# SwiGLU's out-projection as seven block products in a one-core decoder layer

## The chip, the core and the metric

The kernel runs on one core of one Trainium2 chip. The metric is the device time of one execution in microseconds (us), as the median over runs; lower is better. TensorE (PE in the rows) multiplies matrices, VectorE (DVE) and ScalarE (ACT) work element by element, GpSimd (POOL) does some of that too, and SyncE (SP) issues most of the transfers.

## What is computed

One decoder layer over 1024 tokens of width 1024 in float32: RMSNorm, stick-breaking attention with 16 heads, residual; RMSNorm, a SwiGLU network with 2816 hidden columns, residual; a gated add of a per-layer embedding; a last RMSNorm. The part at hand is

```
def swiglu(x, w_in, w_out):
    a, b = jnp.split(x @ w_in, 2, axis=-1)
    return (jax.nn.silu(a) * b) @ w_out
...
h = h + swiglu(rms_norm(h, norm_ffn[i]), ffn_w_in[i], ffn_w_out[i])
gate = jax.nn.sigmoid(rms_norm(h, norm_ple[i]) @ ple_w_gate[i])
```

The change concerns the product with `w_out` (2816 x 1024), called the out-projection below.

## The kernel before

Activations lie transposed: the 128 partitions hold a slice of the width or of the hidden columns, the free dimension holds tokens. Every float32 operand of a matmul is split into two float32r parts, a high part (ScalarE casts the tile) and a low part (VectorE or GpSimd subtracts the high part from the tile). One block product is then three matmuls (`mm3`, lines 126 to 129): high by high, high by low, low by high. A 128 x 1024 split costs one ScalarE and one VectorE instruction, and the VectorE one needs the ScalarE one's result.

The in-projection (lines 843 to 913) runs over 22 hidden tiles `k`; it already computes seven products per tile instead of eight. Its last element-by-element work (`glu`, line 830) multiplies by the sigmoid and stores the activation tile `act_d[k][h]` (128 hidden columns by 512 tokens, `h` is the half of the tokens) to DRAM on SP's queue. For the last tile, `k` = 21, that work is put off into `rest_0` and `rest_1`, which run inside the out-projection.

The out-projection (lines 954 to 988) loops over the two token halves `h` and in each over the 22 hidden tiles `k`. A step loads the 512 KB of weights `w_fo[k]` and the 256 KB of `act_d[k][h]`, splits both (`w_split`, lines 106 to 108: `whi`, `wlo`; `act_split`, lines 626 and 627: `act`), and multiplies them into eight PSUM banks `pm`, one per 128 output columns `m`: 8 x 3 = 24 matmuls of 128 x 512 each. The last two steps of a half are taken bank by bank, and each finished bank gets the residual added (`residual`, line 939, in from DRAM as `h2`) into `hres[m]`. Over both halves that is 2 x 22 x 24 = 1056 matmuls. All of the weights are split twice, once for each half.

The gate projection that follows needs `hres[m]` times its gain, split into `gh[m]` and `gl[m]`, and the sum of squares `acc3` (`parts3`, lines 941 to 952: on ScalarE the high part, line 944, and the square, line 950; on VectorE the low part, line 945; the sum on GpSimd or VectorE, line 952). For the first half of the tokens that runs inside the second half's steps 2 to 9. Five of the eight gate weights `w_g` are split inside the second half too (`WGK`).

The order is written out by hand: under `manual_schedule` every engine executes its instructions in the order in which the program names them, and a tile's buffer is waited for one by one. The pool `xp` has sixteen 512 KB slots (tag X) that hold the split parts.

Of the kernel before, what the change touches and what calls it, by code (L numbers as in the profile page):

```python
# [7 lines left out]
F32 = mybir.dt.float32  # L8
# [24 lines left out]
WGK = [3, 7, 11, 15, 18]  # L33
# [7 lines left out]
def tile_trunk(ctx: ExitStack, tc: tile.TileContext, xT, pT, gains, ident, w_qkv, w_o, w_fi, w_fo, w_g, w_p, outT):  # L41
# [25 lines left out]
    for h in range(2):  # L67
        for k in range(NFF):
            order.append((w_fo[k], KT, k == NFF - 1))
            if h == 1 and k in WGK:  # L70
                order.append((w_g[WGK.index(k)], KT, True))
    for m in range(len(WGK), KT):
        order.append((w_g[m], KT, m < 6))
# [22 lines left out]
    def w_split(k):  # L96
        if k < lim[0] and k in raws:
# [9 lines left out]
            eng = nc.gpsimd if k < N1 or n_fi <= k < n_fi + 2 or k >= len(order) - 3 else nc.vector  # L107
# [514 lines left out]
    def act_split(i):
        if i < 2 * NFF and i not in acts:
            t = araw.pop(i)
            a = duo(xp, f"act{i}", "X", None)
            nc.scalar.copy(a[:, 0, :], t)
            nc.vector.tensor_tensor(a[:, 1, :], t, f(a[:, 0, :]), op=ALU.subtract)  # L627
            acts[i] = a

    with ExitStack() as c2:  # L630
        p2 = c2.enter_context(tc.tile_pool(name="p2", bufs=1, reuse_waits="tile"))

# [210 lines left out]
        for k in range(NFF):  # L843
# [3 lines left out]
            if k >= NFF - 2:  # L847
                for i in range(2):
                    w_load(n_fi + 2 * (k + 2 - NFF) + i)
                act_dma(k + 2 - NFF)  # L850
# [18 lines left out]
            if k == NFF - 1:  # L869
                w_split(n_fi)  # L870
                act_split(0)
# [26 lines left out]
            if k == NFF - 1:  # L898
                act_dma(2)
# [25 lines left out]
        rests = [rest_0, rest_1]  # L925


    p3 = ctx.enter_context(tc.tile_pool(name="p3", bufs=1, reuse_waits="tile"))
    hres = [p3.tile([P, T], F32, name=f"h{m}") for m in range(KT)]
    hh = [p3.tile([P, T], F32R, name=f"gh{m}") for m in range(KT)]  # L930
    hl = [p3.tile([P, T], F32R, name=f"gl{m}") for m in range(KT)]
# [110 lines left out]
    for ri, (c0, n) in enumerate(ranges):  # L1042
# [3 lines left out]
        for m in range(KT):  # L1046
# [3 lines left out]
            for kt in range(KT):  # L1050
                mm3(ps[:, :n], wh[:, kt, :], wl[:, kt, :], hh[kt][:, c0:c0 + n], hl[kt][:, c0:c0 + n], kt == 0, kt == KT - 1)
# [76 lines left out]
```

## Time and profile before

| what | value |
|---|---|
| median of 3 runs | 1380.06 us (1379.49 to 1381.41) |
| profiled execution, its own time | 1380.04 us |
| its span, first to last instruction | 1378.3 us |
| mean granted TensorE clock | 0.996 of full |
| busy, share of the span: PE / DVE / ACT / POOL | 98% / 73% / 44% / 30% |

The profiled execution took what the median run takes, and 1.7 us lie outside its span. Busy shares are averages over stages that have different limits, so each stage is read by itself, from the stretches and the timeline. In the rows below, L108 is line 108; out<-in are the program's names without their numbers; "idle before" is how long the engine stood still before an instruction and what released it. Matmuls overlap: one lasts 389 ns, but the next one starts before it ends.

### The profile page before, as it was taken

The page shows a single profiled execution, that of the slowest core. Times are in us where ns is not written, and L with a number is a line of the kernel's source. Part 1 is how long each engine was busy: PE and PEld are TensorE (multiplying, and loading weights), DVE is VectorE, ACT ScalarE, POOL GpSimd, SP SyncE. Part 2 cuts the span into 40 slices and gives each one's busy share as a digit, 9 for nine tenths or more (in the row PEclk, how much of TensorE's full clock was granted, in tenths as well). Part 3 has the DMA queues.
Part 4 walks back from the last instruction along what each step waited for, and adds up shares of the span by engine and source line. Part 5 has one row for each costly group of instructions (what it writes and reads, how often), then busy time and mean ns, then how long its engine had stood idle before and what let it go on. Part 6 is the DMA issues. An engine that isn't in the chain of part 4 may idle for free. (4 is left out here: it accounts for less than half of the span.)

```text
span 1378.3 us, 17601 instructions
## 1 busy us (share of the span) xinstructions
PE 1353.9 (98%) x6620; PEld 1133.0 (82%) x6620; DVE 1004.1 (73%) x1305; ACT 607.6 (44%) x1082; POOL 408.3 (30%) x280
## 2 busy tenths in 40 slices
PE   8999999999999999999999999999999999999996
PEld 6888888888888888888888888888888888888896
DVE  6878878787887866677878888888884335635675
ACT  6555565656556665443222223222323233534322
POOL 2222221313222401245454544545450000301321
PEclk9999999999999999999999999999999999999998
DMA  5101111110101662442221222212235446455123
GB/s 185 62 16 61 31 48 45 47 47 31 61 31 68 208 237 70 148 143 78 92 92 63 75 92 92 92 62 76 92 138 183 138 143 227 150 181 178 35 72 101
DMA packets 55509, 137.54 MB, mean 100 GB/s; under 512 B 6016, under 2 KB 10496, under 8 KB 55424
## 3 DMA queue, kind: packets, MB, share of 16 engines
q1 hardware_dynamic: 53136, 128.82, 27.2%
q0 software_dynamic: 2016, 7.34, 1.5%
q8 instruction: 52, 0.85, 0.2%
q14 instruction: 33, 0.27, 0.1%
q10 hardware_dynamic: 272, 0.26, 0.1%
HBM read 104.94 MB, written 31.46 MB: 99 GB/s over the span
## 5 line engine op out<-in xcount | busy, mean ns | idle before, releaser
L417 DVE TENSOR_TENSOR_SCAN a<-a,hot 128x128 f32<-128x128 f32 (+7 forms) x128 | 188.8, 1491 | 24.6 <-ACT a L410 24.0
L108 POOL TENSOR_TENSOR wlo<-wraw,whi 128x1024 fp32r<-128x1024 f32 x29 | 72.8, 2516 | 293.3 <-ACT whi L106 117.9
L106 ACT CAST whi<-wraw 128x1024 fp32r<-128x1024 f32 x84 | 88.2, 1051 | 161.8 <-PE b_m L128 144.6
L108 DVE TENSOR_TENSOR wlo<-wraw,whi 128x1024 fp32r<-128x1024 f32 x55 | 69.1, 1257 | 119.6 <-ACT whi L106 119.5
L127 PE MATMUL b_pj<-xh,whi 128*128 128x512 f32 x352 | 140.6, 399 | 0.0
L129 PE MATMUL b_pj<-xh,wlo 128*128 128x512 f32 x352 | 138.7, 394 | 0.4 <-POOL wlo L108 0.4
L128 PE MATMUL b_pj<-xl,whi 128*128 128x512 f32 x352 | 137.8, 391 | 0.0
L440 DVE TENSOR_TENSOR al<-b_tp,ah 128x512 fp32r<-128x512 f32 (+2 forms) x160 | 93.1, 599 | 53.9 <-ACT ah L439 53.5
L439 ACT CAST ah<-b_tp 128x512 fp32r<-128x512 f32 (+2 forms) x160 | 82.0, 522 | 78.7 <-PE b_tp L430 77.8
L410 ACT ACTIVATE a<-b_z 128x128 f32<-128x128 f32 (+2 forms) x192 | 87.0, 491 | 49.0 <-PE b_z L408 47.8
L128 PE MATMUL b_m<-act,whi 128*128 128x512 f32 x264 | 102.8, 389 | 0.4 <-DVE act L627 0.4
L127 PE MATMUL b_m<-act,whi 128*128 128x512 f32 x264 | 102.8, 389 | 0.0
L129 PE MATMUL b_m<-act,wlo 128*128 128x512 f32 x264 | 102.7, 389 | 0.0
L430 PE MATMUL b_tp<-hot,a 128*128 128x128 f32 x576 | 94.3, 273 | 2.5 <-DVE al L440 2.5
L430 PEld LDWEIGHTS b_tp<-hot,a 128*128 128x128 f32 x576 | 72.6, 140 | 25.8 <-DVE al L440 5.5
L129 PEld LDWEIGHTS b_pj<-xh,wlo 128*128 128x128 f32 x352 | 66.0, 188 | 16.2 <-POOL wlo L108 0.5
L128 PEld LDWEIGHTS b_pj<-xl,whi 128*128 128x128 f32 x352 | 66.2, 188 | 8.9
L127 PEld LDWEIGHTS b_pj<-xh,whi 128*128 128x128 f32 x352 | 66.1, 188 | 8.6
L450 PE MATMUL b_av<-ah,V 128*128 128x512 f32 (+2 forms) x160 | 70.7, 442 | 0.0
L952 POOL TENSOR_TENSOR acc<-acc,sq 128x512 f32<-128x512 f32 x10 | 17.6, 1756 | 158.5 <-ACT sq L950 157.8
L832 ACT ACTIVATE sg<-u 128x512 f32<-128x512 f32 x22 | 13.9, 633 | 108.8 <-issue 86.6
L128 PEld LDWEIGHTS b_m<-act,whi 128*128 128x128 f32 x264 | 49.6, 188 | 11.1 <-DVE act L627 0.8
(3040 smaller groups left out, 3745.6 us busy)
## 6 DMA issues: line engine op xcount, KB each, us to landing
fraw<-w_fi SPq DMA_DIRECT2D x44, 512.0 KB, 4.4
wraw<-w_fo SPq DMA_DIRECT2D x44, 512.0 KB, 3.7
wraw<-w_qkv SPq DMA_DIRECT2D x22, 512.0 KB, 3.6
araw<-act SPq DMA_DIRECT2D x44, 256.0 KB, 3.9
h<-h SPq DMA_DIRECT2D x32, 256.0 KB, 3.1
sp<-hl SPq DMA_DIRECT2D x14, 512.0 KB, 3.0
act<-u SPq DMA_DIRECT2D x22, 256.0 KB, 2.2
act<-c SPq DMA_DIRECT2D x22, 256.0 KB, 2.6
```

The source lines that it names most:

```text
L106: nc.scalar.copy(hi[:, :n, :], t[:, :n, :])
L108: eng.tensor_tensor(lo[:, :n, :], t[:, :n, :], f(hi[:, :n, :]), op=ALU.subtract)
L127: nc.tensor.matmul(ps, whi, xhi, start=first, stop=False)
L128: nc.tensor.matmul(ps, whi, xlo, start=False, stop=False)
L129: nc.tensor.matmul(ps, wlo, xhi, start=False, stop=last)
L410: nc.scalar.activation(a[:, c0:c0 + e], z[:, :e], AF.Sigmoid, scale=-SCALE)
L417: nc.vector.tensor_tensor_scan(a[:, L - 1::-1], a[:, L - 1::-1], hot[:, back], 0.0, op0=ALU.mult, op1=ALU.max)
L430: nc.tensor.transpose(b[:, j * P:(j + 1) * P], a[:, kt * P:(kt + 1) * P], idn)
L439: nc.scalar.copy(ah[:, m0:m0 + 512 - j0 * P], b[:, j0 * P:])
L440: nc.vector.tensor_tensor(al[:, m0:m0 + 512 - j0 * P], b[:, j0 * P:], f(ah[:, m0:m0 + 512 - j0 * P]), op=ALU.subtract)
L450: nc.tensor.matmul(ps[:, c0:], o.V[:, kt, hd, :], ah[:, r0:], start=kt == 0, stop=False)
L952: eng.tensor_tensor(acc3[:, hs], acc3[:, hs], s, op=ALU.add)
```

## The change

The out-projection's matrices are cut in two along output columns, hidden columns and tokens: four blocks each of the weights, the activations and the result. Seven products of sums and differences of blocks (`FO`) replace the eight block products. A product is accumulated over 11 hidden tiles `j` in four banks, so a step is 4 x 3 = 12 matmuls of 128 x 512, and there are 77 steps: 924 matmuls.

A step's operands lie side by side in one tile of 2 x 512 columns, the weights (128 hidden by 512 outputs) on the left and the activation (128 hidden by 512 tokens) on the right. So one ScalarE instruction makes both high parts and one VectorE instruction both low parts, 1024 columns each (`fo_hi`, `fo_lo`). P1 takes the blocks as they are. P5, P6 and P7 first form a difference, a difference and a sum of two such tiles on VectorE, 1024 columns in one instruction, kept in `SX[j]` for P5 and P6. P2 takes blocks as they are; P4 and P3 form a difference of 512 columns.

In step `n` the program names the transfers for step `n` + 6, the low parts for step `n` + 2, then the sum or difference and the high parts for step `n` + 3. Each step brings two transfers of 256 KB, and steps 0 to 2 and 5 to 15 a third one for `SX`.

Finished banks are evacuated one per step during the next product (`evac_fo`): ScalarE copies for P1 and P5, one VectorE add for P6, P2, P4 and P3, three VectorE instructions for P7. The residual is no longer added by VectorE out of a loaded tile: GpSimd issues 16 accumulating transfers that add `h2` into `hres`. `parts3` of the first token half runs one per step in steps 5 to 8 of P4 and of P3; its sum goes to VectorE for odd `m`, to GpSimd for even `m`. Five gate weights are loaded ahead and split inside P2. The wait on GpSimd for the first two weight splits (line 107) is gone.

```
-    for h in range(2):
-        pm = [None] * KT
-        tail = []
-        for k in range(NFF):
-            i = h * NFF + k
-            act_dma(i)
-            act_split(i)
-            act_dma(i + 1)
-            act_dma(i + 2)
-            wh, wl = w_next()
-            if h == 1 and 2 <= k < 10:
-                parts3(k - 2, 0)
-            act_split(i + 1)
...
-    def residual(m, h, ps, t):
-        nc.vector.tensor_tensor(hres[m][:, HS[h]], ps, t, op=ALU.add)
+    FO = ("P1", "P5", "P6", "P7", "P2", "P4", "P3")
+    def fo_hi(n):
+        p, j = FO[n // NJ], n % NJ
+        d = fraw.pop(n)
...
+        if p == "P5":
+            tt(SX[j], SX[j], d)
+            d = SX[j]
+        elif p == "P6":
+            tt(SX[j], d, SX[j])
+            d = SX[j]
+        elif p == "P7":
+            tt(d, d, SX[j], ALU.add)
+        elif p == "P4":
+            tt(d[:, 1, :], d[:, 1, :], SX[j][:, 1, :])
+        elif p == "P3":
+            tt(SX[j][:, 0, :], d[0], SX[j][:, 0, :])
+            d = SX[j]
+        hi = duo(xp, f"fh{n}", "X", None)
+        if p == "P1":
+            for q in range(2):
+                nc.scalar.copy(hi[:, q, :], d[q])
+        else:
+            nc.scalar.copy(hi, d)
+        fop[n] = d, hi
+
+    def fo_lo(n):
+        d, hi = fop[n]
+        lo = duo(xp, f"fl{n}", "X", None)
+        if isinstance(d, tuple):
+            for q in range(2):
+                nc.vector.tensor_tensor(lo[:, q, :], d[q], f(hi[:, q, :]), op=ALU.subtract)
+        else:
+            nc.vector.tensor_tensor(lo, d, f(hi), op=ALU.subtract)
+        fop[n] = hi, lo
...
             if k == NFF - 1:
-                w_split(n_fi)
-                act_split(0)
+                fo_prep(0)
...
-            eng = nc.vector if h and m % 2 else nc.gpsimd
+            eng = nc.vector if m % 2 else nc.gpsimd
             eng.tensor_tensor(acc3[:, hs], acc3[:, hs], s, op=ALU.add)
...
+    def residual(m, h):
+        nc.gpsimd.dma_start(hres[m][:, HS[h]], h2_d[m][h], accum_op=ALU.add)
+
+    def evac_fo(p, i, ps):
+        c11, c12 = hres[i][:, HS[0]], hres[i][:, HS[1]]
+        c21, c22 = hres[i + 4][:, HS[0]], hres[i + 4][:, HS[1]]
+        if p == "P1":
+            nc.scalar.copy(c11, ps)
+        elif p == "P5":
+            nc.scalar.copy(c22, ps)
+        elif p == "P6":
+            plus(c21, ps, c11)
+            residual(i, 0)
+        elif p == "P7":
+            plus(c12, c21, c22, ALU.subtract)
+            residual(i, 1)
+            plus(c21, ps, c21, ALU.subtract)
+            plus(c22, c21, c22)
+            residual(i + 4, 1)
+            residual(i + 4, 0)
+        elif p == "P2":
+            plus(c11, ps, c11)
+        elif p == "P4":
+            plus(c21, ps, c21)
+        else:
+            plus(c12, ps, c12)
...
+    for n in range(NS):
+        p, j = FO[n // NJ], n % NJ
+        fo_load(n + 6)
+        if n < 3:
+            nc.sync.dma_start(SX[n][:, 1, :], act_d[n][0])
+        if 5 <= n < 5 + NJ:
+            fo_w(SX[n - 5][:, 0, :], n - 5, 1, 1)
+        fo_lo(n + 2)
+        fo_hi(n + 3)
+        if (p, j) in gate_split:
+            w_split(n_fi + gate_split[(p, j)])
+        if (p, j) in gate_load:
+            w_load(n_fi + gate_load[(p, j)])
+        if j == 0:
+            pm = [mb() for _ in range(4)]
+        hi, lo = fop.pop(n)
+        for i in range(4):
+            ws = slice(i * P, i * P + P)
+            mm3(pm[i], hi[:, 0, ws], lo[:, 0, ws], hi[:, 1, :], lo[:, 1, :], j == 0, j == NJ - 1)
+        if n in (2, 5):
+            rests.pop(0)()
```

The order on VectorE in the middle of the out-projection, before: `wlo` is a weight's low part, `act` an activation's, each with its own ScalarE cast.

```order
L108 TENSOR_TENSOR wlo43_9770<-wraw43_9697,whi43_9769 128x1024
L627 TENSOR_TENSOR act9_9773<-araw_9730,act9_9773 128x512
L108 TENSOR_TENSOR wlo44_9805<-wraw44_9732,whi44_9804 128x1024
L627 TENSOR_TENSOR act10_9808<-araw_9765,act10_9808 128x512
L108 TENSOR_TENSOR wlo45_9840<-wraw45_9767,whi45_9839 128x1024
```

VectorE in the middle of P6 after the change: L646 is the sum or difference of a step, L678 its low part, `fh23` the high part that ScalarE makes of the difference `s1`.

```order
L678 TENSOR_TENSOR fl22_9930<-s0_9444,fh22_9913 128x1024
L646 TENSOR_TENSOR s1_9451<-raw23_9867,s1_9451 128x1024
L678 TENSOR_TENSOR fl23_9950<-s1_9451,fh23_9933 128x1024
L646 TENSOR_TENSOR s2_9458<-raw24_9887,s2_9458 128x1024
L678 TENSOR_TENSOR fl24_9970<-s2_9458,fh24_9953 128x1024
```

Before, a low part followed another low part, and each had its own cast; now the difference of a step, which its cast needs, stands directly ahead of the low part that needs the cast, with nothing between.

VectorE where `parts3` runs, before (second half, steps 2 to 4; L945 is its low part `gl`):

```order
L108 TENSOR_TENSOR wlo59_10362<-wraw59_10281,whi59_10361 128x1024
L945 SCALAR_TENSOR_TENSOR gl0_9462<-h0_9446,gn_67,gh0_9454 128x512
L627 TENSOR_TENSOR act25_10368<-araw_10322,act25_10368 128x512
L108 TENSOR_TENSOR wlo60_10400<-wraw60_10324,whi60_10399 128x1024
L945 SCALAR_TENSOR_TENSOR gl1_9463<-h1_9447,gn_67,gh1_9455 128x512
```

The same after the change, in P4's steps 5 to 7 (L1017 is the low part of `parts3`, L1025 its sum):

```order
L678 TENSOR_TENSOR fl62_10809<-raw62_10718,fh62_10791 128x1024
L646 TENSOR_TENSOR raw63_10741<-raw63_10741,s8_9455 128x512
L1017 SCALAR_TENSOR_TENSOR g_0_0_10826<-h0_9446,gn_67,g_0_0_10826 128x512
L678 TENSOR_TENSOR fl63_10833<-raw63_10741,fh63_10812 128x1024
L646 TENSOR_TENSOR raw64_10764<-raw64_10764,s9_9462 128x512
L1017 SCALAR_TENSOR_TENSOR g_1_0_10850<-h1_9453,gn_67,g_1_0_10850 128x512
L1025 TENSOR_TENSOR acc3_9469<-acc3_9469,sq_10853 128x512
L678 TENSOR_TENSOR fl64_10859<-raw64_10764,fh64_10836 128x1024
```

And ScalarE there after the change (L666 casts a step's high parts, L1016 is the high part of `parts3`, L1020 and L1023 its square):

```order
L666 CAST fh63_10812<-raw63_10741 128x1024
L1016 ACTIVATE g_0_0_10826<-h0_9446,gn_67 128x512
L1020 ACTIVATE acc3_9469<-h0_9446 128x512
L666 CAST fh64_10836<-raw64_10764 128x1024
L1016 ACTIVATE g_1_0_10850<-h1_9453,gn_67 128x512
L1023 ACTIVATE sq_10853<-h1_9453 128x512
```

The low part of `parts3` now stands between a step's difference and its low part, and its high part behind that step's cast on ScalarE.

SP's queue at the start of the out-projection, before and after: `act_21_0` and `act_21_1` are the stores of `rest_0` and `rest_1`.

```order
L93 DMA wraw38_9508<-w_fo 128x1024
L835 DMA act_21_0_5429<-u2_9364 128x512
L620 DMA araw_9548<-act_4_0_5395 128x512
L93 DMA wraw39_9550<-w_fo 128x1024
L835 DMA act_21_1_5430<-c22_9389 128x512
L620 DMA araw_9590<-act_5_0_5397 128x512
```

```order
L891 DMA act_21_0_5429<-u2_9364 128x512
L614 DMA raw_g6_9468<-w_fo 128x512
L636 DMA s9_9462<-act_9_0_5405 128x512
L614 DMA raw10_9576<-w_fo 128x512
L636 DMA s10_9459<-act_10_0_5407 128x512
L614 DMA raw11_9597<-w_fo 128x512
L636 DMA raw11_9597<-act_0_1_5388 128x512
L614 DMA s0_9444<-w_fo 128x512
L891 DMA act_21_1_5430<-c22_9388 128x512
L614 DMA raw12_9626<-w_fo 128x512
```

The transfers for step 9 and later stand behind the first store, those for step 12 and later behind the second.

## Rows read from the trace of the kernel before

**Rows 1.** The page's first part: busy time, share of the span, instructions.

```profile
PE 1353.9 (98%) x6620; PEld 1133.0 (82%) x6620; DVE 1004.1 (73%) x1305; ACT 607.6 (44%) x1082; POOL 408.3 (30%) x280
```

**Rows 2.** A stretch inside the out-projection: busy time by engine, clock, DMA share.

```profile
core 0: us, PE busy (x) PEld busy (x) DVE busy (x) ACT busy (x) POOL busy (x), PEclk, DMA share, GB/s
1080.00:1130.00 50.00, 50.00 (x222) 41.43 (x221) 17.48 (x20) 14.16 (x18) 0.00 (x0) 1.00 0.43 142
```

**Rows 3.** Groups by line, out-projection; TensorE's first of three equal lines.

```profile
L127 PE MATMUL b_m<-act,whi 128*128 128x512 f32 x264 | 102.8, 389 | 0.0
L127 PE MATMUL b_pj<-act,whi 128*128 128x512 f32 x88 | 34.2, 389 | 0.0
```

**Rows 4.** Timeline (start, duration) of TensorE: the out-projection's first, the gate's first.

```profile
1028.54 0.39 PE L127 MATMUL b_m<-act,whi 128*128 128x512 f32 x1
1029.31 0.50 PE L128 MATMUL b_m<-act,whi 128*128 128x512 f32 x1 [0.38 <-DVE act L627]
...
1268.77 0.39 PE L127 MATMUL b_m<-gh,whi 128*128 128x512 f32 x1
```

**Rows 5.** Timeline of ScalarE and VectorE, one step of the out-projection.

```profile
1100.10 1.05 ACT L106 CAST whi<-wraw 128x1024 fp32r<-128x1024 f32 x1 [3.87 <-PE b_m L128]
...
1101.19 1.23 DVE L108 TENSOR_TENSOR wlo<-wraw,whi 128x1024 fp32r<-128x1024 f32 x1 [3.61 <-ACT whi L106]
1102.33 0.68 DVE L627 TENSOR_TENSOR act<-araw,act 128x512 fp32r<-128x512 f32 x1
1106.63 1.23 DVE L108 TENSOR_TENSOR wlo<-wraw,whi 128x1024 fp32r<-128x1024 f32 x1 [3.61 <-ACT whi L106]
```

**Rows 6.** Timeline where the in-projection ends: VectorE, and SP's store.

```profile
1026.47 0.33 SPq L835 DMA_DIRECT2D act<-c  x1
...
1027.68 1.57 DVE L627 TENSOR_TENSOR act<-araw,act 128x512 fp32r<-128x512 f32 x1
...
1029.18 0.68 DVE L634 TENSOR_TENSOR u<-b_pj,u 128x512 f32<-128x512 f32 x1
...
1031.09 0.97 DVE L627 TENSOR_TENSOR act<-araw,act 128x512 fp32r<-128x512 f32 x1
...
1037.69 0.69 DVE L828 TENSOR_TENSOR q<-q,rstd 128x512 f32<-128x512 f32 x1
...
1039.81 0.69 DVE L834 TENSOR_TENSOR u<-q,u 128x512 f32<-128x512 f32 x1
```

**Rows 7.** Lines of `parts3`: durations in ns, least, median and most.

```profile
L944 ACT ACTIVATE gh<-h,gn x16: 707/721/724, 1160.9 to 1308.2; 128x512 fp32r<-128x512 f32 x16
L945 DVE SCALAR_TENSOR_TENSOR gl<-h,gn,gh x16: 744/748/2892, 1162.2 to 1308.9; 128x512 fp32r<-128x512 f32 x16
L950 ACT ACTIVATE sq<-h x14: 617/619/622, 1164.1 to 1308.8; 128x512 f32<-128x512 f32 x14
```

**Rows 8.** Timeline: VectorE beside a sum of `parts3` on GpSimd.

```profile
1178.49 0.75 DVE L945 SCALAR_TENSOR_TENSOR gl<-h,gn,gh 128x512 fp32r<-128x512 f32 x1
...
1178.60 1.78 POOL L952 TENSOR_TENSOR acc<-acc,sq 128x512 f32<-128x512 f32 x1 [3.66 <-ACT sq L950]
1179.15 1.78 DVE L627 TENSOR_TENSOR act<-araw,act 128x512 fp32r<-128x512 f32 x1
```

**Rows 9.** Transfers: rate in 40 slices of 1080 to 1130, issues, GpSimd's own.

```profile
GB/s 0 102 362 172 0 62 295 272 0 0 226 369 34 0 115 354 161 0 29 292 310 11 0 216 379 34 0 121 300 208 0 52 326 251 0 0 170 370 89 0
...
araw<-act SPq DMA_DIRECT2D x9, 256.0 KB, 3.9
```

**Rows 10.** GpSimd's issuing of transfers, attention stage: ns, then us to landing.

```profile
L485 POOL DMA_DIRECT2D ath<-sp x7: 532/570/720, 463.8 to 505.1; - x7
...
DMA to landing us min/median/max: 3.6/9.5/13.3
```

**Rows 11.** Stretches at the kernel's end, columns as in rows 2.

```profile
1362.00:1365.00 3.00, 1.59 (x13) 1.30 (x11) 2.09 (x6) 1.04 (x3) 0.00 (x0) 1.00 0.16 56
1368.00:1371.00 3.00, 0.66 (x2) 0.29 (x2) 1.51 (x10) 0.34 (x1) 0.00 (x0) 0.50 0.00 0
```

More of the change, by code (lines that the diff above doesn't have):

```diff
@@ L32 @@
 MORD = [0, 4, 1, 5, 2, 6, 3, 7]
-WGK = [3, 7, 11, 15, 18]
 def f(ap):
@@ L66, in tile_trunk @@
     n_fi = len(order)
-    for h in range(2):
-        for k in range(NFF):
[L69 to L73, printed above, removed]
+    for m in range(KT):
+        order.append((w_g[m], KT, m > 1))
     N1 = 3 * NPAIR + 2
@@ L106, in w_split @@
             nc.scalar.copy(hi[:, :n, :], t[:, :n, :])
-            eng = nc.gpsimd if k < N1 or n_fi <= k < n_fi + 2 or k >= len(order) - 3 else nc.vector
+            eng = nc.gpsimd if k < N1 or k >= len(order) - 3 else nc.vector
             eng.tensor_tensor(lo[:, :n, :], t[:, :n, :], f(hi[:, :n, :]), op=ALU.subtract)
@@ new lines, in fo_hi, with tt @@
+    def fo_hi(n):
+        if n >= NS:
+            return
+        p, j = FO[n // NJ], n % NJ
+        d = fraw.pop(n)
+        def tt(out, a, b, op=ALU.subtract):
+            nc.vector.tensor_tensor(out, a, b, op=op)
+        if p == "P5":
[8 more added lines that the diff above has]
+            tt(d[:, 1, :], d[:, 1, :], SX[j][:, 1, :])
+        elif p == "P3":
+            tt(SX[j][:, 0, :], d[0], SX[j][:, 0, :])
[7 more added lines that the diff above has]
+        fop[n] = d, hi
@@ L846, in tile_trunk @@
             fi_load(k + 2)
[L847 to L850, printed above, removed]
+            if k == NFF - 1:
+                for n in range(3):
+                    fo_load(n)
             ps1 = prod(w["A11"], "B11")
@@ L925, in tile_trunk @@
         rests = [rest_0, rest_1]
+    ring[1] = None
     p3 = ctx.enter_context(tc.tile_pool(name="p3", bufs=1, reuse_waits="tile"))
-    hres = [p3.tile([P, T], F32, name=f"h{m}") for m in range(KT)]
-    hh = [p3.tile([P, T], F32R, name=f"gh{m}") for m in range(KT)]
-    hl = [p3.tile([P, T], F32R, name=f"gl{m}") for m in range(KT)]
+    hres = [None] * KT
+    for t in ("g0", "s0", "h7", "h0", "s4", "s7", "h3", "g1", "s1", "h6", "h1", "s5", "s8", "h4", "g2", "s2", "s10", "h2", "s6", "s9",
+              "h5", "g3", "s3", "g4", "g5", "g6"):
+        if t[0] == "h":
+            hres[int(t[1])] = p3.tile([P, T], F32, name=t)
+        elif t[0] == "s":
+            SX[int(t[1:])] = p3.tile([P, 2, 512], F32, name=t, tag=t, bufs=1)
+        else:
+            d = p3.tile([P, 2, 512], F32, name=f"raw_{t}", tag=t, bufs=1)
+            n = 3 + int(t[1])
+            fraw[n] = d
+    hh = [[None] * KT, [None] * KT]
+    hl = [[None] * KT, [None] * KT]
     acc3 = row("acc3")
@@ L943, in parts3 @@
         g = gn[:, 2, m:m + 1]
-        nc.scalar.activation(hh[m][:, hs], hres[m][:, hs], AF.Copy, scale=g)
-        nc.vector.scalar_tensor_tensor(hl[m][:, hs], hres[m][:, hs], g, f(hh[m][:, hs]), op0=ALU.mult, op1=ALU.subtract)
-        if m == 0:
+        if h or m < 7:
+            d = p3.tile([P, 2, 512], F32R, name=f"g_{m}_{h}", tag=f"s{m}" if h else f"g{m}", bufs=1)
+        else:
+            d = duo(xp, "g_7_0", "X", None)
+        hh[h][m], hl[h][m] = d[:, 0, :], d[:, 1, :]
+        nc.scalar.activation(hh[h][m], hres[m][:, hs], AF.Copy, scale=g)
+        nc.vector.scalar_tensor_tensor(hl[h][m], hres[m][:, hs], g, f(hh[h][m]), op0=ALU.mult, op1=ALU.subtract)
+        if h not in begun:
+            begun.add(h)
             nc.scalar.activation(acc3[:, hs], hres[m][:, hs], AF.Square)
@@ new lines, in plus @@
+    def plus(out, x, y, op=ALU.add):
+        nc.vector.tensor_tensor(out, x, y, op=op)
+    def residual(m, h):
[3 more added lines that the diff above has]
+        c21, c22 = hres[i + 4][:, HS[0]], hres[i + 4][:, HS[1]]
+        if p == "P1":
+            nc.scalar.copy(c11, ps)
[15 more added lines that the diff above has]
+            plus(c21, ps, c21)
+        else:
+            plus(c12, ps, c12)
@@ new lines, in tile_trunk @@
+    gate_load = {("P6", 8): 0, ("P7", 4): 1, ("P2", 1): 2, ("P2", 3): 3, ("P2", 5): 4, ("P4", 1): 5, ("P4", 2): 6}
+    gate_split = {("P2", 1): 0, ("P2", 3): 1, ("P2", 5): 2, ("P2", 7): 3, ("P2", 9): 4}
+    n_wg = len(gate_split)
+    jobs = []
+    for n in (3, 4, 5):
+        fo_load(n)
+    fo_hi(2)
+    for n in range(NS):
+        p, j = FO[n // NJ], n % NJ
+        fo_load(n + 6)
+        if n < 3:
+            nc.sync.dma_start(SX[n][:, 1, :], act_d[n][0])
[15 more added lines that the diff above has]
+            rests.pop(0)()
+        if j == NJ - 1:
+            jobs += [lambda p=p, i=i, ps=ps: evac_fo(p, i, ps) for i, ps in enumerate(pm)]
+            more = {"P2": range(4), "P4": range(4, KT)}
+            jobs += [lambda m=m: parts3(m, 0) for m in more.get(p, ())]
+        elif j:
+            left = NJ - 1 - j
+            for _ in range(1 if len(jobs) <= left else 2):
+                if jobs:
+                    jobs.pop(0)()
@@ L991, in tile_trunk @@
+    while jobs:
+        jobs.pop(0)()
+    for q in range(n_wg):
+        wg.append(parts.pop(n_fi + q))
+    cur[0] = n_fi + n_wg
     acc4 = row("acc4")
```

83 lines of the change are left out of this document (37 added, 46 removed).

## The prediction

> **What bounds the kernel now.** I read the page's first part, then the stretches, then the timeline. TensorE is busy 98% of the span [rows 1]. In the out-projection it has no gap: 222 matmuls in 50 us at full granted clock, while VectorE is busy 17.5 us, ScalarE 14.2 and GpSimd 0 of the 50 [rows 2]. So this stage is bound by TensorE's matmuls, and VectorE and ScalarE have room. The stage runs from 1028.54 to 1268.77, 240.2 us [rows 4]. Its step of 24 matmuls takes 5.44 us, from 1101.19 to 1106.63 [rows 5], that is 0.2267 us a matmul; 88 groups of 12, 2.72 us each, make 239.4, and the other 0.8 is a halt at its head, where the first low part of an activation comes late, 1028.54 to 1029.31 [rows 4].
>
> What the reader is to see in [rows 5] is the hand-over, because the change makes it matter: the cast runs 1100.10 to 1101.15, the low part starts at 1101.19. ScalarE to VectorE costs 0.04 us. And the next VectorE instruction starts 1.14 us after the low part, not 1.23.
>
> **What the change removes.** 1056 matmuls (264 and 88 on each of three lines) [rows 3] become 924. 132 x 0.2267 = 29.9 us of TensorE's time go, if operands arrive in time. 77 steps x 2.72 = 209.4 us is the floor of the stage.
>
> **What the sums and differences add.** In P5, P6 and P7 each step needs on VectorE a sum (L646) and a low part (L678), both with two inputs in SBUF and 1024 columns, like L108: 1.23 us each [rows 5]. By busy time that is 2.4 us in 2.72. But the order on VectorE is sum 23, low part 23, sum 24, low part 24: low part 23 waits for cast 23, that waits for sum 23, and sum 24 is queued behind low part 23 though its data have long landed. In the middle of the step VectorE stands still for the cast. One round is 1.14 (low part to next start) + 1.23 (sum) + 0.04 + 1.05 (cast) + 0.04 = 3.50 us. TensorE wants a step every 2.72. So 0.78 us per step is lost as soon as the lead is used up. "A step apart" holds in the program's text; on VectorE's queue nothing stands between a sum and the low part that hangs on it.
>
> The Trainium skill (VectorE: DVE Perf Modes, The DRAIN you can't avoid) says that a VectorE instruction does not start before the one ahead has emptied its pipe. By it the round would be 3.59 and the time some 5 us above my sum; [rows 5] show 1.14 for this pair, and I go by them.
>
> **The lead.** How far VectorE is ahead at step 11, the first with a difference, follows from the queue at the head. VectorE is late there already: it comes to the first split at 1027.68, just before TensorE needs it [rows 6]. After the change it does: low part 0 (two halves, to 1029.0), three adds of the in-projection (1.9 us, 1029.18 to 1031.09 in [rows 6]), low part 1 (1.2), two adds and a small one (1.4), low parts 2 to 4 (3.6), rest_0 (2.8, from 1037.69 to the end of 1039.81's instruction), low parts 5 to 7 (3.6), rest_1 (2.8), low parts 8 to 10 (3.6): about 1049.9. The transfers of step 9 and later stand behind rest_0's store, issued near 1039.9; at the 3.9 us of [rows 9] the operands of step 9 are there by 1044. Those of step 12 stand behind rest_1's store near 1046.3, there by 1051, just in time. Then difference 11 and its round: low part 11 is done near 1053.5. TensorE comes to step 11 at 1028.5 + 0.6 (halt at the head, of the kind of the 0.8 now) + 29.9 = 1059.0. The lead is 5.5 us.
>
> Steps 12 to 43 are 32 rounds x 0.78 = 25.0; less the lead, **19.5 us** of halts, all in the last part of P5, in P6 and P7. P6's add into the result (0.68, one a step) falls into VectorE's wait for the cast and costs nothing; were that wait gone, it would cost 4 x 0.6.
>
> **P2** has no sum: low parts 11 x 1.14, P7's evacuation 4 x 2.0, five gate low parts 5 x 1.14, together 26.2 us against 29.9 of TensorE. No halt, and VectorE gains 3.7 us.
>
> **P4 and P3** have a difference of 512 columns: 1.14 + 0.69 + 0.04 + 1.05 + 0.04 = 2.96 us a round, 0.23 too much. P4's first eight rounds take 1.9 of the 3.7, and the last gate split in one of them another 1.0; 0.8 is left. Then `parts3` enters the chain. VectorE's L1017 waits for its high part, which stands behind the step's cast on ScalarE: 0.72 less the 0.09 overlap, then 0.75 less 0.09 [rows 7], so +1.3 us. For odd m the sum of squares on VectorE adds 0.6, for even m (but 0) it is on GpSimd and holds up VectorE: in [rows 8] L627 lasts 1.78 instead of 0.68, until GpSimd is through, +1.1. Seven rounds with `parts3` (m = 0 to 6; m = 7 comes after the last low part) lose 0.23 each as well: 1.5 + 3 x 2.1 + 3 x 2.6 = 15.6. The seven rounds between them lose 1.6. Less the 0.8: **16.4 us** of halts.
>
> **The sum.** 209.4 + 0.6 + 19.5 + 16.4 = 245.9 us for the stage, against 240.2: +5.7. Profiled execution 1380.04 (the median is 1380.06): **1385.5 us**, rounded down, since the halt at the head may fall away.
>
> **What is hidden or has no row.** ScalarE's evacuations (P1, P5) stand between casts, where ScalarE waits for VectorE anyway. Three transfers of 256 KB per step in P5 are 225 GB/s at 3.50 us; the trace has slices at 379 [rows 9], so nothing; at the 142 GB/s of a whole stretch it would be a bound, but there buffers pace the transfers and slices at 0 stand beside those at 379. GpSimd's 16 accumulating transfers: issuing one takes 0.57 us [rows 10], 9 us in all, on an engine with nothing else to do. Accumulation has no row; a plain one of 512 KB landed after 3.6 to 13.3 us [rows 10], and the first to be needed is needed 50 us after its issue, so between 0 and, if the twelve in P2 push the loads back by 13.3 against 3.7 of lead, +10; I take 0, since the loads run six steps ahead. The gate projection starts with its operands ready, like now: its last `parts3` needs 1.4 us on VectorE while TensorE has 2.7 to go; between 0 and the 2.7 us that GpSimd's three weight splits may hold VectorE, I take 0.
>
> **Rivals.**
> *VectorE stays ahead* (faster). If transfers and stores at the head come sooner and the sixteen `xp` slots let casts run six steps ahead, the lead is 6 x 2.72 = 16 instead of 5.5, and GpSimd's sums may miss VectorE (-3.3): 1372. Were the chain broken altogether, 1380 - 30 = 1350. For it: VectorE's busy time fits. Against it: VectorE comes late to the head [rows 6], and the order. It decides from a lead of 14 us.
> *The chain costs what the matmuls give* (no change): 0.03 less per hand-over and sum, a lead of 8: 1380 to 1382.
> *The clock falls* (slower still). At the end a stretch with half the matmuls still has full clock, and after 3 us without one it is at half [rows 11]. The halts here are 0.8 us in 3.5; if the clock fell in them, a step would take 5.1 us and the 20 to 40 halted steps up to 1.6 us more each: 1390 to 1440. The Trainium skill (TensorE: Matmul & The Clock Gate, A second HAM failure mode: psum-queue depth-cycling) describes a kernel in which frequent short idling makes the clock swing; no row before shows such idling.
> *Loads late in P1 and P5* (slower): steps 5 to 15 want 0.8 MB each and SP waits for two stores; with 3.9 us for three transfers a round there, eleven rounds lose 0.4 each: +5, 1391.
>
> **Chances.** The sum as it stands, 1377 to 1394: 0.78, of it 0.53 above 1382.8, 0.24 within, 0.01 below 1377.3. VectorE ahead: 0.12. Clock: 0.05. Loads late beyond the range: 0.05. 0.2% of 1380, 2.8 us, is about what a measurement here can tell from no change. Faster 0.13, same 0.24, slower 0.63. The range 1377 to 1394: low end with no cost on GpSimd (-3.3), a lead of 9 (-3.5) and 0.02 less per round (-1.5); high end with the late loads (+5) and 0.06 more per round (+3.5).
>
> **What would show it.** After the change: 924 matmuls on lines 119 to 121; VectorE's low part L678 starting every 3.5 us from about step 20 to 43, with some 1.1 us of wait for ScalarE's L666 ahead of it; TensorE's waits put down to L678; no halts in P2; rounds of 4.2 to 5.3 us where L1017 stands; granted clock 1.00 throughout. It is wrong if VectorE's rounds in P6 are under 3 us, if TensorE waits for transfers, or if the gate's first matmul comes before 1266 or after 1283.

## The result

The changed kernel takes 1396.66 us, the median of 4 runs (1394.76 to 1397.78), beside 1379.86 us before (4 runs, 1379.49 to 1381.41): a ratio of 1.0117, 95% interval 1.0103 to 1.0130. It is slower, as forecast, but by 16.8 us instead of 5.4, and beyond the range of 1377 to 1394. The profiled execution has a span of 1394.2 us, 15.9 more than before.

The page's first part answers to [rows 1]: 132 matmuls fewer, less busy time of TensorE and more of VectorE, a longer span.

```profile
PE 1342.6 (96%) x6488; PEld 1110.5 (80%) x6488; DVE 1074.8 (77%) x1378; ACT 623.6 (45%) x1090; POOL 408.0 (29%) x290
```

TensorE's timeline (start, duration, operands, in brackets the idle time and what ended it) answers to [rows 4]: the stage's first matmul, two of the halts in P6, the last of P7, the two at the start of P4, three at the end of P3, and the gate projection's first matmul.

```profile
1030.03 0.39 PE L119 MATMUL b_m<-fh 128*128 128x512 f32 x1
...
1102.80 0.50 PE L120 MATMUL b_m<-fl,fh 128*128 128x512 f32 x1 [0.49 <-DVE fl L678]
1106.34 0.50 PE L120 MATMUL b_m<-fl,fh 128*128 128x512 f32 x1 [0.53 <-DVE fl L678]
...
1166.94 0.50 PE L120 MATMUL b_pj<-fl,fh 128*128 128x512 f32 x1 [0.58 <-DVE fl L678]
...
1204.48 0.50 PE L119 MATMUL b_pj<-fh 128*128 128x512 f32 x1 [2.09 <-ACT fh L666]
1207.82 0.80 PE L120 MATMUL b_pj<-fl,fh 128*128 128x512 f32 x1 [2.84 <-DVE fl L678]
...
1272.53 0.50 PE L120 MATMUL b_m<-fl,fh 128*128 128x512 f32 x1 [2.33 <-DVE fl L678]
1277.40 0.50 PE L120 MATMUL b_m<-fl,fh 128*128 128x512 f32 x1 [1.86 <-DVE fl L678]
1282.86 0.50 PE L120 MATMUL b_m<-fl,fh 128*128 128x512 f32 x1 [1.13 <-DVE fl L678]
...
1285.51 0.39 PE L119 MATMUL b_pj<-g,whi 128*128 128x512 f32 x1
```

The stage goes from 1030.03 to 1285.51, 255.5 us against 240.2 in [rows 4]. What comes behind it takes 108.7 us (109.5 before), so the loss lies in the stage, apart from the 1.5 us by which it begins later (the last section tells of them). These lines split it. A step is 2.72 us. From 1030.03, step 43 (P7's last) would reach its second matmul at 1147.2; it does at 1166.94: 19.7 us of halts in P5 to P7. P2 follows without a halt and would end at 1199.35; P4 and P3 need 59.8 us without halts and end at 1285.51: 26.3 us there. 209.4 + 19.7 + 26.3 = 255.4.

The prediction had 0.6, 19.5 and 16.4 us of halts. The surplus is in P4 and P3, and its first part is at their head. VectorE there (timeline, same columns):

```profile
1194.11 1.23 DVE L102 TENSOR_TENSOR wlo<-wraw,whi 128x1024 fp32r<-128x1024 f32 x1 [3.94 <-ACT whi L100]
1195.25 1.22 DVE L678 TENSOR_TENSOR fl<-raw,fh 128x1024 fp32r<-128x1024 f32 x1
1196.39 0.69 DVE L646 TENSOR_TENSOR raw<-raw,s 128x512 f32<-128x512 f32 x1
1198.32 1.23 DVE L678 TENSOR_TENSOR fl<-raw,fh 128x1024 fp32r<-128x1024 f32 x1 [1.25 <-ACT fh L666]
1202.61 0.69 DVE L646 TENSOR_TENSOR raw<-raw,s 128x512 f32<-128x512 f32 x1 [3.06 <-DMA raw<-act]
1205.41 1.23 DVE L102 TENSOR_TENSOR wlo<-wraw,whi 128x1024 fp32r<-128x1024 f32 x1 [2.10 <-ACT whi L100]
```

VectorE waits 3.06 us for an operand's transfer. The 3.94 us ahead of L102, the low part of a gate weight, go back to a transfer too, as ScalarE's timeline shows:

```profile
1192.08 1.05 ACT L666 CAST fh<-raw 128x1024 fp32r<-128x1024 f32 x1 [7.78 <-DMA raw<-act]
1193.03 1.04 ACT L100 CAST whi<-wraw 128x1024 fp32r<-128x1024 f32 x1
```

The weight had landed by 1187.1 (issued at 1180.27, landed after 6.8 us), but its cast L100 stands on ScalarE's queue behind a step's cast L666, which waited 7.78 us for an activation. The transfers of that time (1165 to 1215 us; queues with packets, MB and share of 16 engines' time, then issues with KB each and median us to landing):

```profile
q1 hardware_dynamic: 3785, 7.66, 45.0%
q0 software_dynamic: 1728, 3.15, 34.6%
...
h<-h POOLq DMA_DIRECT2D x12, 256.0 KB, 12.0
```

q0 is GpSimd's queue: the twelve accumulating transfers behind P7. From 1174 to 1206 the sixteen engines are busy without a break (share 1.01). And the line of the activations' loads (L636) of 1170 to 1195 us:

```profile
DMA to landing us min/median/max: 5.1/12.3/14.6
```

From 1160 to 1168 the same loads land after 3.0 to 3.2 us.

### The profile page after: what moved, and what is told of

Same layout as the page of the kernel before. It is cut to its first block, busy times and chain, and to the rows that moved or that the text cites. A ratio compares the mean times of both kernels' runs of the same rounds, so it can differ in the third digit from the quotient of the medians.

```text
span 1394.2 us, 17576 instructions
## 1 busy us (share of the span) xinstructions
PE 1342.6 (96%) x6488; PEld 1110.5 (80%) x6488; DVE 1074.8 (77%) x1378; ACT 623.6 (45%) x1090; POOL 408.0 (29%) x290
## 5 line engine op out<-in xcount | busy, mean ns | idle before, releaser
L102 POOL TENSOR_TENSOR wlo<-wraw,whi 128x1024 fp32r<-128x1024 f32 x27 | 67.1, 2487 | 225.8 <-ACT whi L100 127.0
L120 PE MATMUL b_m<-fl,fh 128*128 128x512 f32 x231 | 94.0, 407 | 11.5 <-DVE fl L678 11.3
L119 PE MATMUL b_m<-fh 128*128 128x512 f32 x231 | 91.9, 398 | 0.0
L121 PE MATMUL b_m<-fh,fl 128*128 128x512 f32 x231 | 91.6, 396 | 0.0
L666 ACT CAST fh<-s 128x1024 fp32r<-128x1024 f32 x33 | 34.7, 1051 | 78.2 <-DVE s L646 71.1
L120 PEld LDWEIGHTS b_m<-fl,fh 128*128 128x128 f32 x231 | 44.2, 191 | 29.9 <-DVE fl L678 21.0
L678 DVE TENSOR_TENSOR fl<-s,fh 128x1024 fp32r<-128x1024 f32 x33 | 42.6, 1291 | 31.9 <-ACT fh L666 31.9
L666 ACT CAST fh<-raw 128x1024 fp32r<-128x1024 f32 x33 | 34.1, 1051 | 70.3 <-DVE raw L646 56.4
L888 ACT ACTIVATE sg<-u 128x512 f32<-128x512 f32 x22 | 13.9, 633 | 107.5 <-issue 91.7
```

Source lines behind the costliest of these rows:

```text
L102: eng.tensor_tensor(lo[:, :n, :], t[:, :n, :], f(hi[:, :n, :]), op=ALU.subtract)
L119: nc.tensor.matmul(ps, whi, xhi, start=first, stop=False)
L120: nc.tensor.matmul(ps, whi, xlo, start=False, stop=False)
L121: nc.tensor.matmul(ps, wlo, xhi, start=False, stop=last)
L666: nc.scalar.copy(hi, d)
L678: nc.vector.tensor_tensor(lo, d, f(hi), op=ALU.subtract)
```

## The experiments

Two theories stand against each other for the loss. One: two separate causes, the order sum, cast, low part on VectorE (P5 to P7, and P4 and P3 with `parts3`), and the accumulating transfers (the head of P4). The other: VectorE's busy time sets the rounds, and the gate's weight loads, 512 KB each into two buffers with SP held up behind them, make the transfers late. Eight kernels tell them apart. The stage is read from each profiled execution, from its first matmul to the gate's first. Each ratio is to runs of the kernel before that were taken beside it: 1379.95 us for e1 to e4, 1379.35 for e5 to e8.

| kernel | median us (lowest to highest) | ratio to before, interval | stage us |
|---|---|---|---|
| before | 1379.86 | | 240.2 |
| changed | 1396.66 (1394.76 to 1397.78) | 1.0117, 1.0103 to 1.0130 | 255.5 |
| e1_sum_ahead | 1352.26 (1351.98 to 1353.21) | 0.9802, 0.9785 to 0.9818 | 212.8 |
| e2_no_residual | 1388.62 (1387.99 to 1389.16) | 1.0063, 1.0048 to 1.0078 | 249.4 |
| e3_plain_residual | 1389.77 (1388.69 to 1390.63) | 1.0071, 1.0056 to 1.0086 | 249.4 |
| e4_residual_late | 1389.61 (1387.56 to 1390.58) | 1.0068, 1.0053 to 1.0083 | 249.7 |
| e5_both | 1348.74 (1347.45 to 1349.70) | 0.9776, 0.9762 to 0.9791 | 209.5 |
| e6_parts3_behind | 1383.77 (1382.67 to 1385.49) | 1.0034, 1.0021 to 1.0047 | 243.2 |
| e7_halves | 1375.73 (1374.88 to 1378.65) | 0.9978, 0.9969 to 0.9987 | 238.2 |
| e8_ahead_p5_p7 | 1362.33 (1361.26 to 1362.68) | 0.9874, 0.9859 to 0.9889 | 222.6 |

### The order on VectorE

**e1_sum_ahead.** `fo_hi` is cut in two: `fo_sum` makes the sum or difference, `fo_hi` only the cast.

```
         fo_lo(n + 2)
+        if n + 4 >= NJ:
+            fo_sum(n + 4)
         fo_hi(n + 3)
```

> Edit to the changed kernel: in a step the sum or difference of step n + 4 is named instead of that of step n + 3, so that on VectorE a step's low part no longer stands right behind the sum whose cast it waits for; the casts and low parts stay where they are. Theory (the order sum, cast, low part makes a round of 3.5 us, and in P4 and P3 of 3.0 to 5.4): a round of VectorE in P6 falls to under 2.72 us (1.14 + 1.14 by its instructions), TensorE has no halts in P5 to P7 (19.7 us now) and next to none of the 16 in P4 and P3 that come from the rounds; the 9 us of late transfers behind P2 may stay in part, since VectorE can now be some five steps ahead. 1351 to 1362. Rival (VectorE and ScalarE slow each other down when they work on the same tiles at once, or the transfers pace the rounds): rounds stay above 3.2 us, 1385 or more.

Measured: 1352.26 us, 44.4 less than the changed kernel, at the theory's low end, with the same 924 matmuls and the same instructions on each engine. VectorE in P6 now (timeline of e1_sum_ahead; L688 is the low part there, L647 the sum):

```profile
1101.07 1.22 DVE L688 TENSOR_TENSOR fl<-s,fh 128x1024 fp32r<-128x1024 f32 x1
1102.20 1.22 DVE L647 TENSOR_TENSOR raw<-raw,s 128x1024 f32<-128x1024 f32 x1
1103.34 1.22 DVE L688 TENSOR_TENSOR fl<-raw,fh 128x1024 fp32r<-128x1024 f32 x1
1104.47 1.22 DVE L647 TENSOR_TENSOR raw<-raw,s 128x1024 f32<-128x1024 f32 x1
```

No idle time stands ahead of any of them, a round is 2.27 us, and TensorE has no halt before 1197. The same place in the changed kernel, ScalarE's cast in between:

```profile
1099.11 1.22 DVE L646 TENSOR_TENSOR s<-raw,s 128x1024 f32<-128x1024 f32 x1
...
1100.44 1.05 ACT L666 CAST fh<-s 128x1024 fp32r<-128x1024 f32 x1 [2.50 <-DVE s L646]
...
1101.52 1.23 DVE L678 TENSOR_TENSOR fl<-s,fh 128x1024 fp32r<-128x1024 f32 x1 [1.19 <-ACT fh L666]
1102.66 1.22 DVE L646 TENSOR_TENSOR s<-raw,s 128x1024 f32<-128x1024 f32 x1
...
1105.06 1.23 DVE L678 TENSOR_TENSOR fl<-s,fh 128x1024 fp32r<-128x1024 f32 x1 [1.18 <-ACT fh L666]
```

The reader is to see the 1.19 us that end with the cast, in every round: 3.54 us from one L678 to the next. It was the order alone; the rival (busy time, or the engines slowing each other) falls.

**e7_halves**, on e4_residual_late (below): cast and low part in two halves in P5 to P7, the order kept.

```
+        elif p in ("P5", "P6", "P7"):
+            for q in range(2):
+                nc.scalar.copy(hi[:, q, :], d[:, q, :])
...
+        elif FO[n // NJ] in ("P5", "P6", "P7"):
+            for q in range(2):
+                nc.vector.tensor_tensor(lo[:, q, :], d[:, q, :], f(hi[:, q, :]), op=ALU.subtract)
```

> Edit to e4_residual_late: in P5, P6 and P7 the cast and the low part are made in two halves of 512 columns, the sum stays whole and stays where it is. VectorE's busy time grows (2 x 0.60 instead of 1.14), but its wait is for half a cast only. Theory (the round is sum, cast, low part in series): 1.23 + 0.04 + 0.62 + 0.04 + 2 x 0.60 = 3.13 us instead of 3.5, so 32 x 0.4 = 13 us less: 1375 to 1379. Rival (VectorE's or ScalarE's busy time, or the number of instructions, sets the round): no gain or a loss, 1389 or more.

Measured: 1375.73 us, 13.9 less than e4_residual_late. VectorE does more and the round is shorter, 3.17 us by these lines (x2: the two halves together):

```profile
1111.70 1.29 DVE L682 TENSOR_TENSOR fl<-s,fh 128x512 fp32r<-128x512 f32 x2 [0.74 <-ACT fh L667]
1112.91 1.22 DVE L646 TENSOR_TENSOR s<-raw,s 128x1024 f32<-128x1024 f32 x1
1114.87 1.29 DVE L682 TENSOR_TENSOR fl<-s,fh 128x512 fp32r<-128x512 f32 x2 [0.74 <-ACT fh L667]
```

So the gain follows the part of the cast that is waited for: with the wait shortened from 1.2 to 0.74 us it is 14 us; the next kernel takes the cast out of the chain. In the profiled execution (1377.79 us, above the median) the stage is only 11.5 us shorter than in e4: there TensorE's clock was at half in the last step, and from that step's second matmul to the gate's first it took 4.22 us (1263.04 to 1267.26), where the changed kernel takes 2.65 (1282.86 to 1285.51).

**e8_ahead_p5_p7**, on e4_residual_late: the sums a step earlier in P5 to P7 alone.

```
-        if n + 4 >= NJ:
+        if NJ <= n + 4 < 4 * NJ:
```

The line with the minus is that of e1_sum_ahead.

> Edit to e4_residual_late: the sums a step earlier in P5, P6 and P7 alone; P4 and P3 keep their order. Theory: the 20.8 us of halts in P5 to P7 go, and VectorE enters P4 with a lead (it can be some five steps ahead, 10 us or more) that takes part of the 19 us of P4's and P3's long rounds: 1355 to 1362. Rival (lead does not carry over, since P4's loads have three buffers and come at VectorE's own pace): 1367 to 1370.

Measured: 1362.33 us, 27.3 less than e4_residual_late, 0.3 above the theory's range. The stage is 222.6 us, 13.2 above the floor of 209.4: of the 21.1 us that e4 loses up to the end of P7 0.3 are left, of the 19.2 in P4 and P3 12.9. VectorE's first low part of P4 is ready 9.9 us before TensorE wants it (1169.38 and 1179.24), in e4 4.2 us (1195.61 and 1199.80): a lead longer by 5.7 us, and 6.3 us less of halts. So the lead carries over, for about as much as it is long.

### The transfers

**e2_no_residual, e3_plain_residual, e4_residual_late** change the residual's 16 transfers alone. In this order:

```
     def residual(m, h):
-        nc.gpsimd.dma_start(hres[m][:, HS[h]], h2_d[m][h], accum_op=ALU.add)
+        pass
```

```
     def residual(m, h):
-        nc.gpsimd.dma_start(hres[m][:, HS[h]], h2_d[m][h], accum_op=ALU.add)
+        nc.gpsimd.dma_start(hres[m][:, HS[h]], h2_d[m][h])
```

```
             plus(c12, c21, c22, ALU.subtract)
-            residual(i, 1)
...
-            residual(i + 4, 1)
             residual(i + 4, 0)
...
+        if p == "P3" and j < 8:
+            residual(j, 1)
```

> Edit to the changed kernel: the 16 accumulating transfers that GpSimd issues are left out, so the residual is missing from the result; all else stays. Theory (the twelve that are issued within 15 us at the start of P2 make the operands' transfers late, 10 to 14 us instead of 3, which takes VectorE's lead of 3.7 us and halts TensorE for 5.5 at the second step of P4): transfers issued in P2 land within 4 to 6 us, no halt of 2 us or more behind P2, 1386 to 1389. Rival (the gate's five weight loads of 512 KB in P2, with only two buffers to land in and SP held up at each, make them late): ScalarE still waits for a weight in P2 and TensorE still halts there, 1394 to 1397.

> Edit to the changed kernel: the same 16 transfers, from the same queue and behind the same waits, but without accumulation: they overwrite their target, so the result is another. Theory (an accumulating transfer takes more of the DMA engines than its bytes: in 1165 to 1215 us 3.15 MB of them took 34.6% of the engines' time, 7.66 MB of the others 45.0%, that is 1.87 times as much for a byte): about half of the 9 us goes, 1390 to 1394. Rival (the bytes alone): 1395 to 1398. Rival (accumulation is slow by latency, not by occupancy): 1387 to 1389, as without the transfers.

> Edit to the changed kernel: of the twelve accumulating transfers behind P7 the eight for the second token half, which nobody reads before P3 ends, are issued in P3's first eight steps instead, where the DMA engines are at 5 to 7%; four stay at the start of P2. Theory: as without them, or a little above: 1387 to 1391, and no cost in P3. Rival (four are enough to make the loads late, or P3's end waits for them): 1393 to 1398.

Measured: 8.0, 6.9 and 7.1 us less than the changed kernel, and no halt at the head of P4 in any of them. The loads' landing (line L636, issued 1170 to 1195 us) in e2, e3 and e4, one kernel after the other:

```profile
DMA to landing us min/median/max: 3.9/4.5/4.8
```

```profile
DMA to landing us min/median/max: 6.1/7.0/8.7
```

```profile
DMA to landing us min/median/max: 4.5/5.6/7.0
```

In e2 the gate's weights are loaded as in the changed kernel and nothing is late, so the rival with the two buffers falls. SP is held up there as well: it issues four of these loads from 1180.29 to 1188.89 in e2 and from 1181.19 to 1190.00 in the changed kernel. So the difference lies in how long a load takes to land, not in when it is issued; whether the transfers would have halted TensorE without that holding up, no run shows. e3 missed: half of the gain was expected to stay away, and nearly all of it came, nearer to the rival by latency (1387 to 1389), because loads that land 7 us after their issue are still in time, 12 to 14 us are not. What decides between occupancy and latency is the engines' share of time. Its own lines of 1165 to 1215 us say what an accumulating transfer costs, beside those of the changed kernel above:

```profile
q1 hardware_dynamic: 4497, 9.24, 53.6%
q0 software_dynamic: 960, 3.15, 16.5%
```

The same 3.15 MB take 16.5% of the engines' time without accumulation and 34.6% with it, 2.1 times as much, and 1728 packets instead of 960.

e4 keeps every transfer and moves eight of them: same gain. From the last halt of P7 to the gate it needs 111.4 us (1167.03 to 1278.45), the changed kernel 118.6 (1166.94 to 1285.51): these 7.2 us are what the eight cost where they stood.

### parts3, and both together

**e6_parts3_behind**, on e4_residual_late: `parts3` between a step's low part and the next difference (`pend` holds the row that the last step would have worked on).

```
         fo_lo(n + 2)
+        while pend:
+            parts3(pend.pop(0), 0)
         fo_hi(n + 3)
```

> Edit to e4_residual_late: a row's parts3 in P4 and P3 is named behind the step's low part and ahead of the next difference, so that its low part runs on VectorE after the wait for the cast instead of lengthening it. Theory (parts3 costs 1.3 us a round because its low part waits for a high part that stands behind the cast on ScalarE): 0.6 us less in each of seven rounds, 1384 to 1387 beside e4_residual_late at 1389.6. Rival (the time of its instructions on VectorE alone counts, wherever they stand): 1389 to 1390.

Measured: 1383.77 us, 5.8 less than e4_residual_late, slightly better than expected. One round with a sum of squares on VectorE (L1025) in e4_residual_late, and one in e6:

```profile
1223.36 0.68 DVE L646 TENSOR_TENSOR raw<-raw,s 128x512 f32<-128x512 f32 x1
1225.91 0.75 DVE L1017 SCALAR_TENSOR_TENSOR g<-h,gn,g 128x512 fp32r<-128x512 f32 x1 [1.87 <-ACT g L1016]
1226.58 0.68 DVE L1025 TENSOR_TENSOR acc<-acc,sq 128x512 f32<-128x512 f32 x1
1227.18 1.22 DVE L678 TENSOR_TENSOR fl<-raw,fh 128x1024 fp32r<-128x1024 f32 x1
1228.32 0.69 DVE L646 TENSOR_TENSOR raw<-raw,s 128x512 f32<-128x512 f32 x1
```

```profile
1222.81 1.23 DVE L678 TENSOR_TENSOR fl<-raw,fh 128x1024 fp32r<-128x1024 f32 x1 [1.16 <-ACT fh L666]
1223.95 0.75 DVE L1017 SCALAR_TENSOR_TENSOR g<-h,gn,g 128x512 fp32r<-128x512 f32 x1
1224.61 0.68 DVE L1025 TENSOR_TENSOR acc<-acc,sq 128x512 f32<-128x512 f32 x1
1225.21 0.69 DVE L646 TENSOR_TENSOR raw<-raw,s 128x512 f32<-128x512 f32 x1
1227.14 1.23 DVE L678 TENSOR_TENSOR fl<-raw,fh 128x1024 fp32r<-128x1024 f32 x1 [1.24 <-ACT fh L666]
```

The wait ahead of L1017 is 1.87 us in the one and gone in the other; what stays is the wait of the low part, 1.16 to 1.24. The round goes from 4.96 us (L646 to L646) to 4.33 (L678 to L678), the 0.6 that was expected. The stage is 6.5 us shorter than in e4, and 1.8 of them come back behind it, where TensorE waits 1.58 us for a VectorE instruction (L144) at 1283.94.

**e5_both**: e1_sum_ahead and e4_residual_late together.

> e1_sum_ahead and e4_residual_late together: the sums a step earlier, and the eight transfers of the second token half in P3. Theory (two separate costs: the round of VectorE, and the accumulating transfers): the 3 us of halts that e1_sum_ahead kept around 1198 to 1209 us go too, the stage comes to within 1 us of its floor of 209.4, 1348.5 to 1350.5. Rival (those halts come from the three buffers that P4's loads share): as e1_sum_ahead, 1351.5 to 1353.

Measured: 1348.74 us, 47.9 less than the changed kernel and 2.2% less than before. The stage (TensorE's first and the gate's first matmul):

```profile
1027.42 0.39 PE L119 MATMUL b_m<-fh 128*128 128x512 f32 x1
...
1236.89 0.39 PE L119 MATMUL b_pj<-g,whi 128*128 128x512 f32 x1
```

209.5 us, against a floor of 209.4. The 29.9 us of fewer matmuls are there in full once nothing else is late. The two gains do not add up (44.4 + 7.1 = 51.5): with its longer lead VectorE already covers part of the late loads in e1, where 3.4 us above the floor were left.

## Why the prediction failed

**Right.** The direction, and the mechanism of P5 to P7: VectorE stands still for the cast in every round and the sum waits behind it. L678 starts every 3.5 us with 1.1 to 1.2 us of wait, TensorE's halts begin at 1085 (step 20), and there are 19.7 us of them, 19.5 forecast. That the two lie so close is partly luck: the stage began 1.5 us late, and that time would otherwise have been halts. The first difference on VectorE starts at 1049.57 (1049.9 forecast), its low part ends at 1053.27 (1053.5). e1, e7 and e8 show that order to be the cause. P2 without a halt, rounds of 4.3 to 5.4 us with `parts3`, and the last part of the kernel nearly as before (0.8 us shorter): right too.

**The step that failed: the sixteen accumulating transfers taken at 0.** The text bounded them by +10 "if the twelve in P2 push the loads back by 13.3 against 3.7 of lead", and took 0 "since the loads run six steps ahead". They did push the loads back, to 12 to 14 us, and cost 7 to 8 us (e2 to e4). Six steps of TensorE are 16 us, but VectorE and ScalarE take the operands three steps before TensorE, and P4's loads wait for one of three buffers, which a low part frees (in the lines above L678 ends at 1199.55; SP issues the next load at 1199.57). The bound was good and stood in the text; it belonged into the range, whose high end was built without it. With it the range would have ended at 1404. One of the prediction's own signs of being wrong came with it: the gate's first matmul stands at 1285.51, after 1283. And TensorE does wait for transfers, by way of ScalarE and VectorE.

**The hand-over from VectorE to ScalarE was mis-sized.** [rows 5] show ScalarE to VectorE, 0.04 us, and I took the same for the other direction. In the lines above the sum ends at 1099.11 + 1.22 = 1100.33 and the cast starts at 1100.44: 0.11; over P5 to P7, P4 and P3 it is 0.03 to 0.17 (once 0.45), in P7 0.15 to 0.16 in nearly every round. Low part 11 ends at 1053.27 and low part 43 at 1166.89: 32 rounds of 3.55 us in the mean instead of 3.50, 1.6 us in all. In P4 and P3 e4 has 19.2 us of halts instead of 16.4. Its last twenty rounds on VectorE take 75.05 us (1200.67 to 1275.72), by the prediction's prices 73.1 (thirteen of 2.96, and 15.6 + 7 x 2.72): 1.9 of these 2.8. The other 0.9 are not taken apart here. The rule that the prediction set aside (the Trainium skill, VectorE: DVE Perf Modes, The DRAIN you can't avoid) has an exception in the same paragraph, for an instruction that is not held; e1's lines, with 1.13 to 1.14 us from one instruction of 1.22 us to the next, agree with the exception.

Together, from 1028.54, where the stage began before: up to the end of P7 20.1 us beyond TensorE's own time were forecast (0.6 + 19.5), and it is 21.2 (1.5 of late start and 19.7 of halts), 1.1 more: the 1.6 of the rounds, less small terms. The halt of 0.6 at the head, which the changed kernel does not have, is no term of its own, since VectorE sets the end of P7. (The kernel before has 0.5 there and not the 0.8 that the prediction read: of the 0.77 us in [rows 4] 0.23 are the first matmul's own.) 5.7 forecast for the stage, + 1.1, + 2.8 in P4 and P3, + 7.2 for the transfers: 16.8. Measured: 1285.51 - 1028.54 - 240.2 = 16.8. What comes behind is 0.8 us shorter, so the spans differ by 15.9; the medians differ by 16.8.

**The rivals.** VectorE staying ahead did not come in the changed kernel; e1 made it so by breaking the chain, and its 1352.26 us lie near the 1350 that the prediction gave for that. Loads late in P1 and P5 did not come. The clock fell, where I had it at 0.05, and the sign "granted clock 1.00 throughout" did not hold: not in the halts of 0.8 us in 3.5, but at the long ones in P4 and P3, where it is at half, 1.2 GHz, from 1207.2 to 1214.0, from 1241.3 to 1244.7 and from 1278.8 to 1282.3. Stretches of the changed kernel:

```profile
1090.00:1120.00 30.00, 25.76 (x103) 18.34 (x101) 19.81 (x17) 11.10 (x13) 0.00 (x0) 1.00 0.50 165
...
1204.00:1207.00 3.00, 0.50 (x1) 0.19 (x1) 1.59 (x2) 1.38 (x2) 0.00 (x0) 1.00 0.21 79
1207.00:1210.00 3.00, 2.18 (x5) 1.79 (x6) 1.76 (x3) 1.04 (x1) 0.00 (x0) 0.53 0.34 97
1210.00:1213.00 3.00, 3.00 (x8) 2.32 (x8) 1.48 (x3) 1.05 (x1) 0.00 (x0) 0.50 0.57 194
```

The columns are those of [rows 2]. The first stretch has 103 matmuls where [rows 2] have 222 in 50 us, 133 in 30, and full clock. In the halts of 2.1 and 2.8 us, with one matmul between them, the clock goes to half. That cost the changed kernel next to nothing. In e4 the clock does not fall at that place, and yet VectorE, which sets the pace, takes the same time from P4's second low part to P3's last: 75.03 us in the changed kernel (1207.77 to 1282.80), 75.05 in e4. And behind each of the three falls TensorE comes to wait for VectorE again (at 1230.57, 1245.92 and 1282.86). [rows 11] do not show the "3 us without one" that the prediction read: between their two stretches (1365 to 1368) lie six matmuls, the longest pause is 2.61 us, up to 1366.61, and the clock is at half from 1366.8. The Trainium skill (TensorE: Matmul & The Clock Gate, A second HAM failure mode: psum-queue depth-cycling) tells of a clock that swings under frequent short idling; the halts of P5 to P7, one in every step, do not show it (1.00).

## What to carry to other kernels

In an order written by hand, name an instruction that another engine's result hangs on ahead of the instruction that waits for that engine: VectorE at 2.3 us of work per 2.7 us was late by 20 us only because a sum stood behind the low part of the step before, and one step's distance in the queue was worth 44 us here. Price an accumulating transfer at about twice a plain one of the same bytes (2.1 times here), and look for a stretch with idle DMA engines for those that nobody needs yet. Where an unseen cost is bounded from two sides, carry the bound into the range, however good the reason for taking the low side.

## What was not expected of the hardware

Accumulating transfers into SBUF took 2.1 times the DMA engines' time of plain ones with the same bytes (34.6% against 16.5% of 16 engines in 50 us for 3.15 MB): 5.5 us of all sixteen engines for a MB, where SP's loads beside them took 2.9 (45.0% for 7.66 MB). The four that e4 leaves at that place took 5.6 (11.7% for 1.05 MB). The Trainium skill (DMA: Bandwidth & Descriptors, SDMA does more than copy) names the adding of two streams among what the DMA engines do; no price stands there, and this one is from these traces.

The clock fell once in a stage that the change does not touch, soon after sixteen matmuls of one column, 1.84 us in all, that both kernels have (from 620.50 before, from 620.11 after). It was at half from 623.5 to 626.9. The stretch of before, then of after:

```profile
620.00:630.00 10.00, 10.00 (x57) 8.59 (x57) 7.67 (x19) 3.48 (x6) 2.89 (x2) 1.00 0.36 107
```

```profile
620.00:630.00 10.00, 10.00 (x49) 8.10 (x48) 7.77 (x19) 3.47 (x6) 2.91 (x2) 0.83 0.35 107
```

That is most of why the out-projection began 1.5 us late in this execution, 1030.03 instead of 1028.54; the eight other kernels, without such a fall, began it from 1027.18 to 1029.10. At the end of P7 nothing of it was left: 1166.94 here and 1167.03 in e4_residual_late, which began at 1028.76. Where VectorE sets the end, TensorE's delay costs nothing. Whether these matmuls made the clock fall, or something else did, stays open, for the kernel before has them at full clock.
